# MLP up-projection of an fp32 two-layer trunk: seven half-size products in place of eight, with other SBUF slots and a shorter weight look-ahead

## Chip, cores and metric

One core of one Trainium2 chip runs the whole program in one launch. The metric is the device time of one execution in microseconds (us), the median over runs. Engines are named as in the profile: PE is TensorE's matmul, PEld its weight load, DVE is VectorE, ACT is ScalarE, POOL is GpSimd, SP issues DMAs.

## The reference

512 tokens of width 1024 go through two residual layers: sparse attention with an MLP, then forgetting attention on a shared K/V with an MLP. Everything is float32. The part that matters here is the MLP, which runs once in each layer:

```
D_MODEL = 1024
SEQ = 512
D_FF = 4 * D_MODEL
...
def sq_relu_mlp(xn, w_up, w_down):
    return jnp.square(jax.nn.relu(xn @ w_up)) @ w_down
...
        h = h + sq_relu_mlp(rms_norm(h, g_mlp[layer]), w_up[layer], w_down[layer])
```

## The kernel before, in words

**Arithmetic.** An fp32 operand is split into a high part (rounded to the PE's fp32r format by an ACT copy) and a low part (the rest). A product of two operands is three matmuls, high by high, high by low and low by high (`mm3`, line 521). A weight tile is 1024 words on each of 128 partitions: SP loads it (`raw`), ACT makes `whi` or `dhi`. The low part comes from DVE (raw minus high), or, for the stages listed in `dl`, from ACT (minus the high part) and a DMA from POOL that adds `raw` onto it (`wlo`, lines 507 to 510). The up-projection is in `dl`, the down-projection isn't.

**The MLP** (`mlp`, line 899) goes over four chunks of 1024 hidden features. In a chunk the up-projection makes eight blocks of 128 features by 512 tokens, each in one PSUM bank called `up`: 8 pieces of the width 1024, 3 matmuls each, 24 matmuls with 512 moving columns (`featprod`, line 552). The first four blocks of the first chunk do the same in two halves of 256 tokens, so that they can start before the last tokens are normed. `relu_done` (line 953) makes relu and square on ACT, into four quadrants `X` (256 tokens by 512 features). The down-projection of the chunk multiplies these quadrants by quadrants of `w_down` already with seven products in place of eight (Strassen's scheme in Winograd's form): sums and differences of quadrants on DVE, `dhi`/`dlo` and `xhi`/`xlo` as operands, banks called `tp`, results added into the residual `h` on DVE.

**The order of the work** is written by a list scheduler when the program is built (`schedule`, line 237): each operation has a due time on PE's clock, a table of costs says how long it takes, and the ready operation with the earliest due time goes next on its engine. On the chip each engine then runs its own list in order, and waits on semaphores. A tile takes a slot of SBUF from an arena by its size (`slots` in `CFG`); a weight tile may take one only so many us ahead of PE's clock (`ahead`: raw 40, high 30, low 30).

Of the kernel before, what the change touches and what calls it, by code (L numbers as in the profile page):

```python
# [85 lines left out]
class VTile:  # L86
    _ids = {}

    def __init__(self, pool, shape, dt, name, quota=None):
        n = int(np.prod(shape[1:]))  # L90
        self.words = max(64, 1 << (n - 1).bit_length())

        self.store = pool.arena[self.words] if pool.arena else pool
        self.res = [(p, 1) for p in (self.store, quota) if p is not None]
        self.first = self.end = None
        self.pool, self.shape, self.dt, self.name = pool, tuple(shape), dt, name
        self.real, self.last, self.reads, self.left, self.held, self.by = None, {}, {}, 0, False, {}
# [28 lines left out]
class Recorder:  # L126
# [22 lines left out]
    def add(self, eng, fn, a, k):  # L149
# [21 lines left out]
        if fn == "matmul" and k.get("start"):  # L171
            for p in set(outs[0].t.last.values()):
                op.preds[p] = 1
        for v in outs:
# [62 lines left out]
    def schedule(self):  # L237
# [13 lines left out]
        for o in reversed(ops):  # L251
            for s in o.succ:
                c = (2.0 if o.eng != "POOL" else 5.0) + o.cost if o.fn == "dma_start" else o.cost + self.LAT.get((o.eng, s.eng), 0.1)
                o.prio = min(o.prio, s.prio - c)
# [26 lines left out]
        while done < len(ops):  # L281
# [4 lines left out]
            for e in names:  # L286
# [70 lines left out]
                if o.fn == "dma_start":  # L357
# [3 lines left out]
                    o.end = dma[0] + (1.0 if e != "POOL" else 2.5)  # L361
# [68 lines left out]
def body(ctx, tc, a, out):  # L430
# [14 lines left out]
    def apool(name):  # L445
# [3 lines left out]
        apool(n) for n in ("x8", "h", "wr", "wh", "wl", "s2", "bt", "s4", "ws"))  # L449
    p_ps = pool("ps", 8, bass.MemoryType.PSUM, reach=CFG["ps"])  # L450
    p_dr = {n: pool(n, 1, bass.MemoryType.DRAM) for n in ("hd", "cd")}
# [30 lines left out]
    cosT = const([128, NT, 64], "cosT")  # L482
    sinT = const([128, NT, 64], "sinT")
# [16 lines left out]
    def wunit(src, shape):  # L500
        n = int(np.prod(shape[1:]))
# [90 lines left out]
    def norm_T(src, r, g, xT, t):  # L592
        for i in range(2):
# [6 lines left out]
            c = slice(128 * t, 128 * t + 128)  # L600
            for k in range(2):
                split(xT[0][2 * i + k][:, :, c], xT[1][2 * i + k][:, :, c], b[:, 2 * k:2 * k + 2, :])
# [76 lines left out]
    def unpair(dst, b, scale):  # L679

        up, dn = slice(0, 64), slice(64, 128)
        S.activation(dst[up, 0], b[up], AF.Copy, scale=scale)
# [42 lines left out]
    masks = [scr([128, 128 * (t + 1)], "mask") for t in range(NT)]  # L725
# [85 lines left out]
    oT = new_xT("oT")  # L811
    topk(1)
    qprod(1, 0)
    for t in range(NT):
# [3 lines left out]
        for kv in range(4):  # L818
# [38 lines left out]
            else:  # L857

                pv, u, o = bank([128, 4, 128], "pv"), scr([64, 4, 128], "u"), scr([128, 2, 128], "o")
# [6 lines left out]
            split(oT[0][kv][:, :, c], oT[1][kv][:, :, c], o)  # L866
# [16 lines left out]
    mT = None  # L883

    def proj_o(oT, w, g, first):
        tokprod(xl(oT), w, 0, 8, 0, 512, addto(0), order=first)
        xT = new_xT()

        def last(t, b):
            addto(512)(t, b)  # L890
            norm_T(h[t], rstd(h[t]), g, xT, t)
        tokprod(xl(oT), w, 0, 8, 512, 512, last, order="t")
        return xT

    lows("oa")
    xT = proj_o(oT, a["w_o_a"][0], g, "t")


    def mlp(xT, wu, wd, after, last=False):
        lows("up1" if last else "up0")  # L900
        H = T // 2
        tl = [slice(0, H), slice(H, T)]

        share = [htile([128, 512], "share") for _ in range(2)]

        def add(o, b, x):
            V.tensor_tensor(o, b, x, op=OP.add)

        def xop(src):
            out = []  # L910
            for k in range(0, 4, 2):
                hl = tuple(rec.tile(p_x8, [128, 2, H], F32R, n) for n in ("xhi", "xlo"))
                split(hl[0], hl[1], src[:, k:k + 2, :])
                out.append(hl)
            return out

        def wop(src):
            out = []
            for y in src:
                hl = rec.tile(p_wh, [128, 2, 512], F32R, "dhi"), rec.tile(p_wl, [128, 2, 512], F32R, "dlo")  # L920
                split(hl[0], hl[1], y)
                out.append(hl)
            return out

        def sub(o, p, q):
            for x, y, z in zip(o, p, q):
                V.tensor_tensor(x, y, z, op=OP.subtract)

        def part(b, x, w, start, i, c=slice(0, 512), js=range(2)):

            for j in js:
                for k in (2 * j, 2 * j + 1):
                    mm3(b[:, c], tuple(u[:, k % 2, 128 * i:128 * i + 128] for u in x[j]),
                        tuple(u[:, k % 2, c] for u in w[j]), start and k == 0, k == 3, skip_group_check=True)

        def prod(bs, x, w, start, whole=False):
            if whole:
                for i in range(2):
                    part(bs[i], x, w, start, i)
            else:  # L940
                for j in range(2):
                    for i in range(2):
                        part(bs[i], x, w, start, i, js=(j,))

        def banks():
            return [bank([128, 512], "tp") for _ in range(2)]

        for ci in range(4):
# [11 lines left out]
            if ci == 0:  # L960
                us = [wS(wu, 128 * i) for i in range(4)]
                bs = [bank([128, T], "up") for _ in range(4)]
                for half in range(2):
                    for i in range(4):
                        featprod(xT, us[i], bs[i], tl[half])
# [3 lines left out]
            for f in range(f, 8):  # L969
                b = bank([128, T], "up")  # L970
                featprod(xT, wS(wu, f0 + 128 * f), b)
                relu_done(f, b)


            def raw(j, n):
                ys = []
                for k in range(f0 + 512 * j, f0 + 512 * j + 512, 256):
                    ys.append(rec.tile(p_wr, [128, 2, 512], F32, "raw"))
                    SP.dma_start(ys[-1], wd[k:k + 256, 512 * n:512 * n + 512].rearrange("(k p) c -> p k c", p=128))
                return ys  # L980
# [10 lines left out]
            prod(a, xop(X[0, 0]), w11, True)  # L991
# [5 lines left out]
            prod(a, xop(X[0, 1]), wop(raw(1, 0)), False)  # L997
# [6 lines left out]
            prod(b, xop(s1), wop(y11), True)  # L1004
# [8 lines left out]
            prod(d, xop(s1), wop(y11), True)  # L1013
# [4 lines left out]
            prod(b, xop(X[0, 1]), wop(y22), False, lastc)  # L1018
# [7 lines left out]
            prod(c, xop(X[1, 0]), wop(y12), True)  # L1026
# [5 lines left out]
            x22 = xop(X[1, 1])  # L1032
# [20 lines left out]
    xq, xk = new_xT(), new_xT()  # L1053

    def afterA(t):
# [6 lines left out]
        if t % 2:  # L1062
            c = slice(128 * t - 128, 128 * t + 128)
            for k in range(0, 8, 2):
# [5 lines left out]
                for x, g in ((xq, gq), (xk, gkv)):  # L1070
                    for i in range(2):
                        split(x[0][k // 2][:, i, c], x[1][k // 2][:, i, c], b[:, i, :], scale=g[:, k + i:k + i + 1])

    ys = {}
    mlp(xT, a["w_up"][0], a["w_down"][0], afterA)
# [32 lines left out]
    lows("v")  # L1108

    vb = [[big([128, 8, 2, 64], "vb") for _ in range(2)] for _ in range(NT)]  # L1110
    vbf = {(t, p): htile([128, 128], "vbf") for t in range(NT) for p in CFG["pvb"]}
    for n in range(2):
        def vdone(t, b, n=n):
            for p in CFG["pvb"]:
                if p // 4 == n:
                    S.copy(vbf[t, p], b[:, 128 * (p % 4):128 * (p % 4) + 128])
            split(vb[t][n][:, :, 0, :], vb[t][n][:, :, 1, :], b.heads(64))
        tokprod(xl(xk), wkv, 0, 8, D + 512 * n, 512, vdone)
# [34 lines left out]
    def kproj(p):  # L1153
# [3 lines left out]
        ks = [htile([128, 2, T], "kdup", F32R) for _ in range(2)]  # L1157
        for e in range(2):
# [7 lines left out]
    def bias(hd_):  # L1166
        ck = scr([128, T], "ck")
        SP.dma_start(ck, cd.row(hd_))
        bt = [rec.tile(p_bt, [128, 128 * (t + 1)], F32, "bt") for t in range(NT)]
        for t in range(NT):  # L1170
            n = 128 * (t + 1)
            G.tensor_scalar(bt[t], ck[:, :n], -1.0, cq[:, t, hd_:hd_ + 1], op0=OP.mult, op1=OP.add)
            dg = bt[t][:, n - 128:n]
            G.affine_select(dg, dg, pattern=[[-1, 128]], compare_op=OP.is_ge, fill=NEG, base=0, channel_multiplier=1)
        return bt

    def attn(p, ks, bts):
        pts = {}
        for e in range(2):
# [4 lines left out]
            ls = {}  # L1184
            for t in CFG["bord"]:
# [4 lines left out]
                l, mn = scr([128, n], "l"), small(1, "mn")  # L1190
# [43 lines left out]
        else:  # L1234
            o = scr([128, T], "o")
# [9 lines left out]
        split(qo[p][:, 0, :], qo[p][:, 1, :], o)  # L1245

    kss = {0: kproj(0)}
    bts = {hh: bias(hh) for hh in range(2)}
    for p in range(8):
        if p < 7:  # L1250
            kss[p + 1] = kproj(p + 1)
        attn(p, kss[p], [bts[2 * p], bts[2 * p + 1]])
        if p < 7:
            for hh in (2 * p + 2, 2 * p + 3):
                bts[hh] = bias(hh)
# [8 lines left out]
    def ol(k, t):  # L1264
        return tuple(qo[k][:, i, 128 * t:128 * t + 128] for i in range(2))

    lows("ob")
    tokprod(ol, a["w_o_b"][0], 0, 8, 0, 512, addto(0), order="k")
    xT = new_xT()

    def lastB(t, b):
        addto(512)(t, b)
        norm_T(h[t], rstd(h[t]), g, xT, t)
    tokprod(ol, a["w_o_b"][0], 0, 8, 512, 512, lastB, order="t")
# [21 lines left out]
    mlp(xT, a["w_up"][1], a["w_down"][1], afterB, last=True)  # L1296
# [35 lines left out]
```

## Time and profile before

| | before |
|---|---|
| time, 3 runs | 1168.31 us median (1167.87 to 1169.01) |
| profiled execution | 1168.06 us, of which the span of its instructions 1166.2 us |
| PE busy | 1141.8 us, 98% of the span |
| DVE busy | 771.8 us, 66% |
| ACT busy | 741.6 us, 64% |
| POOL busy | 236.5 us, 20% |
| DMA | 187.86 MB in all, mean 161 GB/s |

A matmul's end is modelled in the profile and successive matmuls overlap, so the price of one in a stream is read from the distance of two starts, and the same holds for DVE and ACT instructions that follow each other at once. All instructions go through one helper, so they stand under one line (L416) and are told apart by tile names, out<-in.

### The profile page before, as it was taken

What the parts mean: (1) busy time and instruction counts of PE and PEld (TensorE: products, weight loads), DVE (VectorE), ACT (ScalarE), POOL (GpSimd) and SP (SyncE); (2) the same over time, 40 slices, a digit from 0 to 9 for tenths busy, and PEclk for the clock granted to TensorE, in tenths of its full rate; (3) what the DMA queues carried; (4) which work ended last, traced back from release to release, by engine and by line L of the source; (5) the groups of instructions that cost most, each with busy time, mean ns of one, the idle gap of its engine ahead of it and who ended that gap; (6) DMA issues with size and microseconds to landing.
All of it is one profiled execution on the core that took longest, in us unless ns stands there. A gap on an engine that the chain in (4) does not pass through costs nothing. (4 is left out here: it accounts for less than half of the span.)

```text
span 1166.2 us, 16382 instructions
## 1 busy us (share of the span) xinstructions
PE 1141.8 (98%) x5687; PEld 948.6 (81%) x5687; DVE 771.8 (66%) x1489; ACT 741.6 (64%) x1396; POOL 236.5 (20%) x391
## 2 busy tenths in 40 slices
PE   8999999999999999999999999999999999999997
PEld 7777787898888888888887878788988888888885
DVE  7899998455736656468656359773568357465596
ACT  8852899665745556559573259996568356465562
POOL 0311454110200200201010068961101002002001
PEclk9999999999999999999999999999999999999999
DMA  9841363782982964957875313768719819739501
GB/s 341 184 91 55 110 181 70 148 235 59 241 242 64 256 186 123 269 150 176 234 173 124 110 37 115 207 169 179 204 68 240 248 56 248 219 88 255 198 19 73
DMA packets 145315, 187.86 MB, mean 161 GB/s; under 512 B 8104, under 2 KB 92096, under 8 KB 145232
## 3 DMA queue, kind: packets, MB, share of 16 engines
q1 hardware_dynamic: 129680, 130.18, 35.5%
q0 software_dynamic: 15552, 56.63, 25.2%
q8 instruction: 45, 0.74, 0.3%
q14 instruction: 38, 0.31, 0.1%
HBM read 125.94 MB, written 4.23 MB: 112 GB/s over the span
## 5 line engine op out<-in xcount | busy, mean ns | idle before, releaser
L416 PE MATMUL up<-xT,whi 128*128 128x512 f32 (+1 forms) x1152 | 323.7, 366 | 0.0
L416 PEld LDWEIGHTS up<-xT,whi 128*128 128x128 f32 x1152 | 207.9, 189 | 34.9
L416 POOL DMA_DIRECT2D wlo<-raw x108 | 95.1, 881 | 692.6 <-ACT wlo L416 339.2
L416 DVE TENSOR_TENSOR dlo<-raw,dhi 128x1024 fp32r<-128x1024 f32 x112 | 136.5, 1227 | 144.5 <-ACT dhi L416 90.3
L416 PE MATMUL up<-xT,wlo 128*128 128x512 f32 (+1 forms) x576 | 210.0, 366 | 0.0
L416 PE MATMUL tp<-dhi,xhi 128*128 128x512 f32 (+1 forms) x452 | 171.9, 390 | 1.2 <-DVE h L416 0.8
L416 PE MATMUL tp<-dlo,xhi 128*128 128x512 f32 (+1 forms) x452 | 171.4, 387 | 0.0
L416 PE MATMUL tp<-dhi,xlo 128*128 128x512 f32 (+1 forms) x452 | 170.8, 388 | 0.0
L416 ACT CAST whi<-raw 128x1024 fp32r<-128x1024 f32 (+2 forms) x124 | 123.9, 1026 | 72.9 <-DMA raw<-in_w_up_dram 63.1
L416 ACT CAST dhi<-raw 128x1024 fp32r<-128x1024 f32 x112 | 116.4, 1047 | 67.1 <-PE up L416 64.1
L416 PE MATMUL tp<-whi,xT 128*128 128x512 f32 (+2 forms) x432 | 125.2, 371 | 2.7 <-DVE r L416 1.6
L416 ACT ACTIVATE wlo<-whi 128x1024 fp32r<-128x1024 f32 x108 | 112.4, 1059 | 20.8 <-DMA wlo<-raw 10.3
L416 PEld LDWEIGHTS up<-xT,wlo 128*128 128x128 f32 x576 | 108.3, 189 | 17.5
L416 DVE TENSOR_TENSOR h<-tp,h 128x512 f32<-128x512 f32 (+1 forms) x97 | 64.7, 680 | 79.0 <-PE tp L416 78.9
L416 PEld LDWEIGHTS tp<-dhi,xhi 128*128 128x128 f32 x452 | 84.8, 188 | 21.7 <-DVE h L416 1.4
L416 PEld LDWEIGHTS tp<-dhi,xlo 128*128 128x128 f32 x452 | 84.7, 188 | 17.3
L416 PEld LDWEIGHTS tp<-dlo,xhi 128*128 128x128 f32 x452 | 84.9, 188 | 16.8
L416 PEld LDWEIGHTS tp<-whi,xT 128*128 128x128 f32 x432 | 77.0, 188 | 14.7 <-ACT whi L416 3.4
L416 DVE TENSOR_TENSOR raw<-raw 128x1024 f32<-128x1024 f32 x64 | 76.6, 1220 | 18.3 <-DMA raw<-in_w_down_dram 17.6
L416 ACT ACTIVATE r<-up 128x512 f32<-128x512 f32 x64 | 37.9, 592 | 79.6 <-PE up L416 79.6
L416 POOL TENSOR_SCALAR l<-l,rc 128x128 f32<-128x128 f32 (+3 forms) x128 | 69.9, 574 | 52.7 <-DVE rc L416 38.3
L416 PE MATMUL tp<-wlo,xT 128*128 128x512 f32 (+2 forms) x216 | 78.4, 372 | 0.5 <-DVE ra L416 0.5
(191 smaller groups left out, 1928.7 us busy)
## 6 DMA issues: line engine op xcount, KB each, us to landing
wlo<-raw POOLq DMA_DIRECT2D x108, 512.0 KB, 8.8
raw<-in_w_down_dram SPq DMA_DIRECT2D x96, 512.0 KB, 10.9
raw<-in_w_up_dram SPq DMA_DIRECT2D x64, 512.0 KB, 7.1
raw<-in_w_kv_b_dram SPq DMA_DIRECT2D x16, 512.0 KB, 6.8
raw<-in_w_in_a_dram SPq DMA_DIRECT2D x12, 512.0 KB, 8.6
raw<-in_w_o_a_dram SPq DMA_DIRECT2D x8, 512.0 KB, 4.4
raw<-in_w_q_b_dram SPq DMA_DIRECT2D x8, 512.0 KB, 7.6
ck<-cd SPq DMA_DIRECT2D x16, 256.0 KB, 3.7
```

Source lines behind the costliest of these rows:

```text
L416: getattr(self.engs[o.eng], o.fn)(*a, **k)
```

## The change

Per MLP, the 28 blocks of the up-projection behind the first four are made four at a time (`quad7`): 512 features by 512 tokens is cut in 2 by 2 by 2, with 256 features, 256 tokens and half of the width 1024, and seven products of that size are made in place of eight. A product is 2 feature blocks, 4 pieces of the width and 3 matmuls, 24 matmuls with 256 moving columns, into one bank. The weights' side needs four sums per quad on DVE (128 x 1024 each) and high and low parts of seven operands in place of four tiles (low parts of three by POOL's DMA, of four by DVE). The tokens' side needs four differences and their high and low parts once per MLP (`tsums`); for these `norm_T` also writes an fp32 copy `xf` of the normed tokens. Results are combined by five DVE additions of 128 x 512 and one ACT copy per quad; the copy after product 1 and the additions after products 6, 5 and 7 read a bank into which the next product then goes on adding.

The SBUF arena has two slot sizes, 44 of 1024 words and 20 of 512, in place of five sizes; small tiles now take a 512 slot, and some are packed together (masks, `l`, the bias tiles of two heads, cos and sin). The MLP's weight tiles may be taken 22 us (raw) and 13 us (high, low) ahead in place of 40 and 30. The scheduler's table lands a DMA 4 us (SP) or 3.5 us (POOL) after its transfer, in place of 1 and 2.5. The new functions `proj7`, `proj_o` and the options `swap` and `dup` are not reached: `p7` is empty and the other two are off.

```
-        self.words = max(64, 1 << (n - 1).bit_length())
+        self.words = 512 if n <= 512 else 1024
...
-    "ahead": {"wr": 40, "wh": 30, "wl": 30},
-    "slots": {1024: 41, 512: 18, 256: 7, 128: 8, 64: 1}, "sizes": (8, 8, 8, 8), "sq": 'S', "x8": 400, "h": 200, "wr": 1500,
+    "land": 4.0, "pw": 700, "p7": (), "swap": False, "dup": False, "ufar": ("1", "2", "4"),
+    "far": ("v3", "v7", "v4"),
+    "mahead": {"wr": 22, "wh": 13, "wl": 13}, "ahead": {"wr": 40, "wh": 30, "wl": 30},
+    "slots": {1024: 44, 512: 20}, "sizes": (8, 8, 8, 8), "sq": 'S', "x8": 400, "h": 200, "wr": 1500,
...
+            split(xT[i, t // 2][0][:, :, c], xT[i, t // 2][1][:, :, c], b)
+            S.copy(xf[i, t // 2][:, :, c], b)
...
+        def tsums():
+            tokside("1", xf[0, 0], xf[0, 1], xf[0, 0])
+            tokside("3", xf[0, 1], xf[1, 1], xf[0, 1])
+            tokside("2", xf[1, 1], xf[1, 1], xf[0, 0])
+            tokside("4", xf[1, 0], xf[1, 0], xf[1, 1])
...
+            def mul(b, w, x, start):
+                for m in range(2):
+                    for k in range(4):
+                        mm3(b[:, H * m:H * m + H], tuple(u[:, k, 128 * m:128 * m + 128] for u in w),
+                            (x(k, 0), x(k, 1)), start and m + k == 0, k == 3, skip_group_check=True)
...
+            mul(b, op(a11, "1"), xd(0, 0), True)
+            m1 = scr([128, T], "r")
+            S.copy(m1, b)
+            a12 = raw(0, 1)
+            mul(b, op(a12, "2"), xd(1, 0), False)
+            done(0, 0, b)
+            s1 = rec.tile(p_mr, [128, 4, 256], F32, "s1")
+            V.tensor_tensor(s1, a21, a22, op=OP.add)
+            V.tensor_tensor(a21, a11, a21, op=OP.subtract)
+            V.tensor_tensor(a11, s1, a11, op=OP.subtract)
+            e = new()
+            mul(e, op(a11, "6"), xs("2"), True)
+            p21 = sumt(e, m1)
+            mul(e, op(s1, "5"), xs("1"), False)
+            p22 = sumt(e, m1)
+            V.tensor_tensor(a12, a12, a11, op=OP.subtract)
+            mul(e, op(a12, "3"), xd(1, 1), False)
+            V.tensor_tensor(m1, e, m1, op=OP.add)
+            done(0, 1, m1)
+            b = new()
+            mul(b, op(a21, "7"), xs("3"), True)
+            V.tensor_tensor(p22, b, p22, op=OP.add)
+            done(1, 1, p22)
+            mul(b, op(a22, "4"), xs("4"), False)
+            V.tensor_tensor(p21, b, p21, op=OP.add)
+            done(1, 0, p21)
...
-            for f in range(f, 8):
-                b = bank([128, T], "up")
-                featprod(xT, wS(wu, f0 + 128 * f), b)
-                relu_done(f, b)
...
+                quad7(f0 + 128 * f, qdone)
```

What this does to the engines' lists shows at three places. The first is PE's list in the up-projection of the first MLP; `up_` with a number is a PSUM bank, `whi`/`uhi` a high part and `wlo`/`ulo` a low part of weights, `xT` and `t` the tokens' side. Before, one block follows the other:

```order
L416 MATMUL up_4076<-xT_2931,wlo_3802 128x512
L416 MATMUL up_4117<-xT_2908,whi_3825 128x512
L416 MATMUL up_4117<-xT_2914,whi_3825 128x512
L416 MATMUL up_4117<-xT_2908,wlo_3835 128x512
L416 MATMUL up_4117<-xT_2908,whi_3825 128x512
```

Now the end of product 6 (bank up_3964) is followed by a piece of product 7 (bank up_4026), and then by the start of product 5, again in bank up_3964:

```order
L423 MATMUL up_3964<-t_3211,uhi_3909 128x256
L423 MATMUL up_3964<-t_3251,uhi_3909 128x256
L423 MATMUL up_3964<-t_3211,ulo_3921 128x256
L423 MATMUL up_4026<-t_3185,uhi_3933 128x256 x2
L423 MATMUL up_4026<-t_3238,uhi_3933 128x256 x2
L423 MATMUL up_4026<-t_3185,ulo_3959 128x256 x2
L423 MATMUL up_4026<-t_3185,uhi_3933 128x256 x2
L423 MATMUL up_4026<-t_3238,uhi_3933 128x256
L423 MATMUL up_3964<-t_3172,uhi_3876 128x256
L423 MATMUL up_3964<-t_3206,uhi_3876 128x256
```

So each matmul is half as wide, and nine matmuls of another product stand between two products that share a bank.

The second place is DVE's list in the same chunk. Before, there is only work of the down-projection:

```order
L416 TENSOR_TENSOR dlo_3515<-raw_3253,dhi_3486 128x1024
L416 TENSOR_TENSOR s1_3541<-sq_3274,sq_3423 128x1024
L416 TENSOR_TENSOR xlo_3552<-sq_3420,xhi_3537 128x512
L416 TENSOR_TENSOR sq_3274<-sq_3267,sq_3274 128x1024
L416 TENSOR_TENSOR xlo_3571<-s1_3541,xhi_3555 128x512
```

Now, for the quad whose banks are shown above, it makes weight sums (`s1`, `raw`), low parts (`ulo`) and the additions out of the banks (`r<-up`):

```order
L423 TENSOR_TENSOR ulo_3959<-raw_3659,uhi_3933 128x1024
L423 TENSOR_TENSOR s1_3974<-raw_3861,raw_3863 128x1024
L423 TENSOR_TENSOR raw_3861<-raw_3784,raw_3861 128x1024
L423 TENSOR_TENSOR raw_3784<-s1_3974,raw_3784 128x1024
L423 TENSOR_TENSOR r_4037<-up_3964,r_3968 128x512
L423 TENSOR_TENSOR xlo_4044<-sq_4013,xhi_4021 128x512
L423 TENSOR_TENSOR ulo_4053<-s1_3974,uhi_4032 128x1024
L423 TENSOR_TENSOR ulo_4067<-raw_3784,uhi_4048 128x1024
L423 TENSOR_TENSOR raw_3806<-raw_3806,raw_3784 128x1024
L423 TENSOR_TENSOR r_4094<-up_3964,r_3968 128x512
```

The addition `r_4037<-up_3964` is what product 5 waits for, and it stands in line behind three sums of 1024 words.

The third place is DVE's list at the end of the program, where `v`, `r` and `hg` are the final norm of two finished token blocks. Before:

```order
L416 TENSOR_TENSOR h<-tp,h 128x512 x2
L416 TENSOR_TENSOR hg<-h,g 128x512
L416 TENSOR_TENSOR v<-ss 128x1
L416 TENSOR_TENSOR hg<-h,g 128x512
L416 TENSOR_TENSOR v<-ss 128x1
L416 TENSOR_SCALAR v<-v 128x1 x2
L416 SCALAR_TENSOR_TENSOR v<-v 128x1 x2
L416 TENSOR_SCALAR v<-v 128x1 x2
L416 TENSOR_TENSOR r<-v 128x1 x2
L416 TENSOR_SCALAR hg<-hg,r 128x512 x2
L416 TENSOR_TENSOR h<-tp,h 128x512
```

Now the last product's low parts stand behind that norm:

```order
L423 SCALAR_TENSOR_TENSOR v<-v 128x1 x2
L423 TENSOR_SCALAR v<-v 128x1 x2
L423 TENSOR_TENSOR r<-v 128x1 x2
L423 TENSOR_SCALAR hg<-hg,r 128x512 x2
L423 TENSOR_TENSOR dlo<-raw,dhi 128x1024
L423 TENSOR_TENSOR xlo<-sq,xhi 128x512
L423 TENSOR_TENSOR dlo<-raw,dhi 128x1024
L423 TENSOR_TENSOR xlo<-sq,xhi 128x512
L423 TENSOR_TENSOR h<-tp,h 128x512
```

Two `dlo` and two `xlo` moved from ahead of the norm to behind it.

## Rows read from the trace of the kernel before

**Rows 1.** The page: span, and busy time, share and instructions of each engine.

```profile
span 1166.2 us, 16382 instructions
...
PE 1141.8 (98%) x5687; PEld 948.6 (81%) x5687; DVE 771.8 (66%) x1489; ACT 741.6 (64%) x1396; POOL 236.5 (20%) x391
```

**Rows 2.** Chain that ended last, second MLP: start us, us, what.

```profile
872.95 37.73 PE tp L416 x166
...
911.59 43.07 PE up L416 x190
```

**Rows 3.** PE's up-projection by shape: count, busy us, mean ns, idle before.

```profile
L416 PE MATMUL up<-xT,whi 128*128 128x512 f32 x896 | 276.9, 389 | 0.0
L416 PE MATMUL up<-xT,wlo 128*128 128x512 f32 x448 | 174.3, 389 | 0.0
L416 PE MATMUL up<-xT,whi 128*128 128x256 f32 x256 | 46.8, 284 | 0.0
```

**Rows 4.** Timeline of PE, first four blocks of the second MLP.

```profile
834.80 0.40 PE L416 MATMUL up<-xT,whi 128*128 128x256 f32 x2
...
845.24 0.40 PE L416 MATMUL up<-xT,whi 128*128 128x256 f32 x2
```

**Rows 5.** Weight loads of the up-projection, all shapes of matmul together.

```profile
L416 PEld LDWEIGHTS up<-xT,whi 128*128 128x128 f32 x1152 | 207.9, 189 | 34.9
```

**Rows 6.** Engines in three chunks of the second MLP (first, third, last and end).

```profile
832.00:911.00 79.00, 79.00 (x426) 68.50 (x425) 48.35 (x57) 47.36 (x72) 6.12 (x7) 1.00 0.70 183
993.00:1075.00 82.00, 82.00 (x363) 67.65 (x362) 47.83 (x54) 46.87 (x68) 7.00 (x8) 1.00 0.69 184
1075.00:1166.00 91.00, 82.21 (x371) 67.60 (x369) 60.55 (x92) 42.45 (x84) 6.75 (x5) 0.98 0.32 103
```

**Rows 7.** Timeline of DVE, instructions of one kind that follow each other.

```profile
394.95 1.28 DVE L416 TENSOR_TENSOR h<-tp,h 128x512 f32<-128x512 f32 x2
...
433.57 3.49 DVE L416 TENSOR_TENSOR raw<-raw 128x1024 f32<-128x1024 f32 x3
```

**Rows 8.** DVE and ACT groups by shape: busy us, mean ns, idle before.

```profile
L416 DVE TENSOR_TENSOR raw<-raw 128x1024 f32<-128x1024 f32 x64 | 76.6, 1220 | 18.3 <-DMA raw<-in_w_down_dram 17.6
L416 DVE TENSOR_TENSOR h<-tp,h 128x512 f32<-128x512 f32 x95 | 63.8, 686 | 79.0 <-PE tp L416 78.9
...
L416 ACT CAST whi<-raw 128x1024 fp32r<-128x1024 f32 x116 | 118.8, 1046 | 72.9 <-DMA raw<-in_w_up_dram 63.1 <-DVE h L416 4.9 <-DMA wlo<-raw 2.1
```

**Rows 9.** Timeline: a bank read by DVE, and PE going on in it.

```profile
1145.40 0.61 PE L416 MATMUL tp<-dhi,xlo 128*128 128x512 f32 x2
...
1145.83 1.29 DVE L416 TENSOR_TENSOR h<-tp,h 128x512 f32<-128x512 f32 x2 [2.07 <-PE tp L416]
...
1156.24 0.41 DVE L416 TENSOR_TENSOR h<-tp,h 128x256 f32<-128x256 f32 x1
...
1156.71 0.39 PE L416 MATMUL tp<-dhi,xhi 128*128 128x256 f32 x1 [0.83 <-DVE h L416]
```

**Rows 10.** DMA issues: count, KB each, median us from issue to landing.

```profile
wlo<-raw POOLq DMA_DIRECT2D x108, 512.0 KB, 8.8
raw<-in_w_down_dram SPq DMA_DIRECT2D x96, 512.0 KB, 10.9
raw<-in_w_up_dram SPq DMA_DIRECT2D x64, 512.0 KB, 7.1
```

**Rows 11.** Engines in two stretches outside the MLPs (first attention, second attention).

```profile
100.00:200.00 100.00, 99.08 (x542) 78.16 (x542) 93.80 (x288) 81.08 (x208) 44.11 (x74) 1.00 0.40 109
...
700.00:790.00 90.00, 87.90 (x503) 72.43 (x502) 75.00 (x202) 87.45 (x211) 72.04 (x154) 1.00 0.58 165
```

**Rows 12.** Timeline of DVE at the end, behind the final norm of two token blocks.

```profile
1150.47 0.68 DVE L416 TENSOR_TENSOR h<-tp,h 128x512 f32<-128x512 f32 x1
...
1152.89 0.69 DVE L416 TENSOR_TENSOR h<-tp,h 128x512 f32<-128x512 f32 x1 [1.02 <-PE tp L416]
...
1154.72 0.69 DVE L416 TENSOR_TENSOR h<-tp,h 128x512 f32<-128x512 f32 x1 [0.41 <-PE tp L416]
```

More of the change, by code (lines that the diff above doesn't have):

```diff
@@ L173, in add @@
                 op.preds[p] = 1
+        if fn == "matmul":
+            t = outs[0].t
+            if k.get("start"):
+                t.begun = op
+            elif t.begun is not None:
+                op.preds[t.begun] = 1
         for v in outs:
@@ L882, in body, with add, xop, pieces @@
     g = gain(a["g_mlp"][0])
[L883 to L887, printed above, removed]
+    def add(o, b, x):
+        V.tensor_tensor(o, b, x, op=OP.add)
+    def xop(src):
+        out = []
+        for x in src:
+            hl = tuple(rec.tile(p_x8, [128, 2, H], F32R, n) for n in ("xhi", "xlo"))
+            split(hl[0], hl[1], x)
+            out.append(hl)
+        return out
+    def pieces(x):
+        return [x[:, 0:2, :], x[:, 2:4, :]]
@@ new lines, in wop, with each @@
+    def wop(src, far=False):
+        out = []
+        for y in src:
+            hl = rec.tile(p_mh, [128, 2, 512], F32R, "dhi"), rec.tile(p_ml, [128, 2, 512], F32R, "dlo")
+            if far:
+                S.copy(hl[0], y)
+                S.activation(hl[1], f32(hl[0]), AF.Copy, scale=-1.0)
+                G.dma_start(hl[1], y, accum_op=OP.add)
+            else:
+                split(hl[0], hl[1], y)
+            out.append(hl)
+        return out
+    def each(op, o, p, q):
+        for x, y, z in zip(o, p, q):
+            V.tensor_tensor(x, y, z, op=op)
@@ new lines, in sub, with part, prod @@
+    def sub(o, p, q):
+        each(OP.subtract, o, p, q)
+    def part(b, x, w, start, i, c=slice(0, 512), js=range(2)):
+        for j in js:
+            for k in (2 * j, 2 * j + 1):
+                mm3(b[:, c], tuple(u[:, k % 2, 128 * i:128 * i + 128] for u in x[j]),
+                    tuple(u[:, k % 2, c] for u in w[j]), start and k == 0, k == 3, skip_group_check=True)
+    def prod(bs, x, w, start, whole=False):
+        if whole:
+            for i in range(2):
+                part(bs[i], x, w, start, i)
+        else:
+            for j in range(2):
+                for i in range(2):
+                    part(bs[i], x, w, start, i, js=(j,))
@@ L889, in last, with proj_d @@
+    quad = lambda x: {(i, j): [x[2 * j + k][:, :, tl[i]] for k in range(2)] for i in range(2) for j in range(2)}
+    def proj_d(lhs, w, g, order):
+        tokprod(lhs, w, 0, 8, 0, 512, addto(0), order=order)
+        xT, xf = new_xq()
         def last(t, b):
             addto(512)(t, b)
[L891 to L899, printed above, removed]
-        lows("up1" if last else "up0")
-        H = T // 2
-        tl = [slice(0, H), slice(H, T)]
-        share = [htile([128, 512], "share") for _ in range(2)]
[L906 to L946, printed above, removed]
@@ L1053, in body @@
     xq, xk = new_xT(), new_xT()
+    xv = [big([128, 2, T], "xv", F32) for _ in range(4)] if "v" in CFG["p7"] else None
     def afterA(t):
@@ L1262, in body, with ol @@
     g = gain(a["g_mlp"][1])
[L1264 to L1274, printed above, removed]
+    if oB:
+        xT, xf = proj_o(quad(oB), a["w_o_b"][0], g, "ob")
+    else:
+        def ol(k, t):
+            return tuple(qo[k][:, i, 128 * t:128 * t + 128] for i in range(2))
+        lows("ob")
+        xT, xf = proj_d(ol, a["w_o_b"][0], g, "k")
     gl = {}
```

281 lines of the change are left out of this document (225 added, 56 removed).

## Prediction

> **What bounds the kernel now.** I read the page first: PE is busy for 1141.8 of 1166.2 us, 98%, while DVE stands at 66% and ACT at 64% [rows 1]. A busy PE need not be a full PE, so the second view is the chain that ended last: in the second MLP it is PE alone, 43.07 us of 190 up-projection matmuls and 37.73 us of 166 down-projection matmuls [rows 2]. That is 0.2267 and 0.2273 us per matmul of 512 columns, back to back. The windows agree: PE fills all of a chunk's 82 us, DVE 47.8 and ACT 46.9 of them [rows 6]. So in the MLPs time is the number of matmuls by their distance, and whatever takes matmuls away shortens the chunk, as long as no other engine grows past it.
>
> **What the change removes.** The trace has 896 + 448 = 1344 up-projection matmuls of 512 columns [rows 3]; all of them lie in the blocks that are rewritten, 14 quads of four blocks (14 x 4 x 24 = 1344). At 0.2267 us they take 304.7 us.
>
> **What it adds on PE.** A quad now has 7 products of 24 matmuls of 256 columns, so 14 x 168 = 2352. The price of one is in this trace, because the first four blocks are made in halves of 256 tokens by the same three-matmul helper, with a weight load for each matmul. In the second MLP a run of them shows high, high, low in a steady beat: from the start at 834.80 to that at 845.24 there are 29 such triples, 87 matmuls, in 10.44 us [rows 4], so 0.1200 us each. 2352 x 0.1200 = 282.2 us. The saving is 22.4 us. It is much less than the eighth that the count of multiplications promises (38 us), because half a matmul costs 53% of a whole one. The point from which it saves nothing is 304.7 / 2352 = 0.1296 us, only 8% above the price.
>
> That margin makes the weight load the first thing to doubt. A load is 189 ns long in the rows [rows 5], longer than the 120 ns of a half-size matmul, yet in [rows 4] every matmul has its load and the beat stays at 0.120, so loads are hidden there, and the new products have the same sequence of loads and widths. The Trainium skill, "TensorE: Matmul & The Clock Gate", in Part 3 under "What overlaps and what doesn't", says that a weight load overlaps matmuls in flight only when it goes to other rows of the array, which full 128-row weights never do. By it the loads would lie bare, twice as many of them, and the change would lose; [rows 2, 4] do not agree with it, and the sum goes by the rows.
>
> **What it adds elsewhere.** DVE: per quad four sums and four low parts of 1024 words and five additions of 512. Those that follow each other start (3.49 - 1.22) / 2 = 1.135 and 1.28 - 0.68 = 0.60 us apart [rows 7, 8], so 8 x 1.135 + 5 x 0.60 = 12.1 us a quad, 24.2 us a chunk. By the whole duration of a row (1.220 and 0.686, [rows 8]) it would be 26.4 us; that is the upper bound, and the lower value is the one that a busy line pays. A middle chunk becomes 82 - 2 x 1.6 = 78.8 us long, with 47.8 + 24.2 = 72.0 us of DVE (91%; 94% by the upper bound). The first chunk, with one quad and the tokens' four differences and low parts (8 x 1.135 = 9.1 us), comes to 48.4 + 12.1 + 9.1 = 69.6 of 77.4 us [rows 6]. ACT: per quad three more casts (1.05 us, [rows 8]), one negation less and a bank copy of about 0.6, so at most 7.5 us a chunk, 54.4 of 78.8. POOL has one DMA less per quad. None of them passes PE, so I book them at nothing, with PE as their cover; DVE's cover is thin, and it is the first rival below.
>
> Turnarounds: four times a quad a bank is read between two products that add into it. From [rows 9], the read starts 0.43 us after the start of the bank's last matmul (the first of the two at 1145.40, to 1145.83), takes about 0.69 [rows 8], and PE starts 0.06 after its end (1156.65 to 1156.71): the price is 0.95 us behind the 0.23 of the matmul itself. PE's list has at least nine half-size matmuls of another product in that place, 1.08 us, so 0.13 us is left where DVE is free at once. I take 1 us in all for those of the 56 turnarounds where it isn't (lower bound nothing; upper bound in the rivals).
>
> Look-ahead: a raw weight lands 7.1 or 10.9 us after its issue, POOL's addition 8.8 [rows 10]. 22 and 13 us ahead still cover one landing each; the DMA traffic doesn't grow. I book nothing.
>
> The end: two `dlo` and two `xlo` now stand behind the final norm of two token blocks, 2 x 1.135 + 2 x 0.60 = 3.5 us more between the first addition at 1145.83 and the last product's additions. DVE idles there for 1.02 + 0.41 = 1.43 us [rows 12], so PE gets its last operands about 2.0 us later, and at the end nothing hides that: 2.0 us lost. Bounds: 0 if PE's other work reaches that far, 3.5 if the idle time isn't usable.
>
> Outside the MLPs the matmuls stay the same; slots and due times shift the order. PE lacks 0.9 of 100 us in the first attention and 2.1 of 90 in the second [rows 11], so there is little to win; a loss of the same size, twice over, is my bound: -3 to +5, taken as 0.
>
> **The sum**, against the profiled execution's own 1168.06 us (span 1166.2 and 1.9 around it): -22.4 + 1.0 + 2.0 = -19.4, so 1148.7. The median of the runs lies 0.25 above that execution, so I forecast 1149 us.
>
> **The rivals.**
> - *DVE becomes the bound.* At 91 to 94% it has 4.6 to 6.8 us a chunk to spare, and it runs its list in order: an addition out of a bank that comes ready while a 1024-word sum runs waits up to 1.14 us for it, and PE then waits as well. There are 3 x 14 = 42 turnarounds through DVE; if each is late by that, 48 us go and the time is about 1197. It decides from 19.4 / 42 = 0.46 us on average. For it: the list shows `r<-up` right behind three such sums. Against it: 9% is idle, and PE's list has matmuls of another product in every turnaround.
> - *Weights come late.* If the shorter look-ahead lets a ninth of a landing of 8.8 us show in each quad, 1 us, 14 us go: about 1163. For it: raw weights now go through a DVE sum before their casts. Against: in the trace PE has no wait for weights in the MLP, and 22 us is twice the longest landing.
> - *The loads show.* If a half-size matmul can't go below its load's 189 ns [rows 5], 2352 x 0.189 = 444.5 us, 140 more than before: 1308. That is also what the Trainium skill's rule would come to, in kind. Against: the beat of [rows 4].
> - *The saving doesn't arrive in full, by many small waits,* half of it lost: about 1158.
> - *The other stages gain*, by 3 us or more, from DMAs issued earlier and more large slots: below 1143.
>
> **How the numbers follow.** The sum, with its bounds (0 to 3.5 at the end, 0 to 3 at the turnarounds, -3 to +5 elsewhere), holds 1143 to 1155: chance 0.68. Half or more of the saving lost to late DVE or late weights, 1155 to 1166: 0.17; nearly all of it, within 0.2% (2.3 us, about what a measurement of this kernel can tell from no change): 0.03. Slower: 0.07, of which DVE as the bound 0.05, the loads 0.01 and weights 0.01. Below 1143: 0.05. So faster 0.90, the same 0.03, slower 0.07. The range takes the likeliest case and the near part of the second: 1142 to 1160.
>
> **What would show it.** Right: an `up` group of 2352 matmuls of 256 columns whose starts are 0.120 us apart, PE without idle time in the middle chunks, a chunk of about 79 us, DVE about 72 us busy in it, and PE waiting for DVE once near the end by about 2 us. Wrong: PE idle in the MLP with `r<-up` or `ulo` on DVE as its releaser (the first rival), or with `raw` or `ulo` landings (the second), or a beat above 0.130 (the third).

## The result, and the profile after

The changed kernel takes 1158.77 us (median of 4 runs, 1157.49 to 1160.14) beside 1168.55 for the kernel before in the same session: a ratio of 0.9916, 95% interval 0.9904 to 0.9928. That is 9.8 us faster, half of the 19.4 that the prediction's sum gave, and inside its range. The profiled execution is the slowest of the four, 1160.14 us.

The page of the kernel after, beside [rows 1]:

```profile
span 1158.3 us, 18559 instructions
...
PE 1126.7 (97%) x6695; PEld 981.4 (85%) x6695; DVE 958.7 (83%) x1671; ACT 788.3 (68%) x1390; POOL 225.2 (19%) x377
```

DVE has 187 us more to do, PE 15 us less. The up-projection by shape, beside [rows 3] (count, shortest, median and longest ns, first and last start), and two starts from PE's timeline:

```profile
L423 PE MATMUL up<-t,uhi x896: 277/283/387, 269.0 to 1104.5; 128*128 128x256 f32 x180
L423 PE MATMUL up<-xT,uhi x672: 277/283/387, 266.1 to 1099.8; 128*128 128x256 f32 x168
L423 PE MATMUL up<-t,ulo x448: 278/283/283, 269.2 to 1104.8; 128*128 128x256 f32 x150
L423 PE MATMUL up<-xT,ulo x336: 274/283/283, 266.4 to 1100.1; 128*128 128x256 f32 x168
```

```profile
1097.30 0.64 PE L423 MATMUL up<-xT,uhi 128*128 128x256 f32 x4
...
1100.17 0.40 PE L423 MATMUL up<-t,ulo 128*128 128x256 f32 x2
```

The four counts add up to 2352. Between the two starts lie 24 matmuls in 2.87 us, 0.1196 each: the forecast price. The second MLP in four windows, each from the first `up` of a chunk to that of the next, the last to the end of the program, and then three windows of 4 us near the end (columns as in [rows 6]):

```profile
821.08:898.17 77.09, 77.09 (x514) 71.09 (x512) 71.47 (x83) 55.18 (x81) 4.36 (x5) 1.00 0.60 167
898.17:977.34 79.17, 79.00 (x506) 71.90 (x505) 70.82 (x80) 51.50 (x67) 5.25 (x6) 1.00 0.64 173
977.34:1056.60 79.26, 79.13 (x505) 71.92 (x504) 71.61 (x81) 51.40 (x67) 5.22 (x6) 1.00 0.65 173
1056.60:1158.30 101.70, 87.26 (x541) 78.10 (x539) 87.30 (x120) 54.86 (x91) 10.21 (x8) 0.95 0.37 109
...
1132.00:1136.00 4.00, 3.01 (x14) 2.16 (x12) 3.55 (x7) 2.70 (x6) 0.00 (x0) 1.00 0.00 0
1136.00:1140.00 4.00, 2.09 (x7) 1.24 (x7) 4.00 (x15) 1.87 (x6) 0.00 (x0) 1.00 0.30 112
1140.00:1144.00 4.00, 3.89 (x12) 3.06 (x12) 3.60 (x6) 0.00 (x0) 0.00 (x0) 0.57 0.43 155
```

The two middle chunks take 79.2 us, where the same starts were 81.76 us apart before, and DVE is busy for 70.8 and 71.6 of them. In the window to the end PE stands still for 14 us, and the granted clock is 0.95. PE's waits (us in all, times, longest), of which all but the second belong to the MLPs:

```profile
PE up L423 <- DVE r L423: 2.7, 5, 1.1
PE tp L423 <- DVE r L423: 1.8, 1, 1.8
...
PE tp L423 <- DVE dlo L423: 1.6, 1, 1.6
...
PE tp L423 <- DVE v L423: 1.3, 1, 1.3
...
PE tp L423 <- DVE h L423: 0.5, 1, 0.5
```

The second was there before as well, with 1.6 us. PE waits for DVE twice near the end (`v`, `dlo`), and right behind that it runs 4 us at a granted clock of 0.57, near the lower of its two levels (1.2 of 2.4 GHz): 12 matmuls there instead of 18 (4 / 0.227).

Where the two executions differ, by the starts of the first and last matmuls of a stage:

| stretch | before, us | after, us | difference | forecast |
|---|---|---|---|---|
| start to the first `up` | 240.32 | 242.12 | +1.8 | 0 |
| from there to the first `up` of the second MLP | 585.56 | 578.96 | -6.6 | -10.7 |
| from there to the last matmul | 332.24 | 326.56 | -5.7 | -8.7 |
| last matmul to the last instruction | 8.01 | 10.62 | +2.6 | 0 |

The forecast column shares the 22.4 and the 1.0 us of the sum evenly and puts the 2.0 us of the end in the third row. The +1.8 in the first row differs from execution to execution: a kernel below (end_order) whose lists are the same up to the first MLP reached it at 240.26. The work isn't shared out quite as before either: behind the program's last `up` 149 matmuls of 512 columns start where 156 did, so 1.6 us of the end's work (7 x 0.227) now lie further ahead.

### The profile page after: what moved, and what is told of

Read it like the earlier page. It is cut to its first block, busy times and chain, and to the rows that moved or that the text cites. A ratio compares the mean times of both kernels' runs of the same rounds, so it can differ in the third digit from the quotient of the medians.

```text
span 1158.3 us, 18559 instructions
## 1 busy us (share of the span) xinstructions
PE 1126.7 (97%) x6695; PEld 981.4 (85%) x6695; DVE 958.7 (83%) x1671; ACT 788.3 (68%) x1390; POOL 225.2 (19%) x377
## 5 line engine op out<-in xcount | busy, mean ns | idle before, releaser
L423 PE MATMUL up<-t,uhi 128*128 128x256 f32 x896 | 146.4, 283 | 0.1
L423 POOL DMA_DIRECT2D ulo<-raw x42 | 36.7, 873 | 526.1 <-ACT ulo L423 336.5
L423 PEld LDWEIGHTS up<-t,uhi 128*128 128x128 f32 x896 | 126.1, 192 | 0.9 <-DVE r L423 0.3
L423 PE MATMUL up<-xT,uhi 128*128 128x256 f32 x672 | 117.7, 284 | 2.7 <-DVE r L423 2.7
L423 DVE TENSOR_TENSOR raw<-raw 128x1024 f32<-128x1024 f32 x92 | 110.6, 1218 | 4.0 <-DMA ulo<-raw 3.3
L423 PEld LDWEIGHTS up<-xT,uhi 128*128 128x128 f32 x672 | 99.8, 191 | 4.9 <-DVE r L423 3.9
L423 PE MATMUL up<-t,ulo 128*128 128x256 f32 x448 | 95.2, 283 | 0.0
L423 ACT CAST uhi<-raw 128x1024 fp32r<-128x1024 f32 x84 | 85.1, 1047 | 13.4 <-DVE raw L423 8.1
L423 PE MATMUL up<-xT,ulo 128*128 128x256 f32 x336 | 80.7, 283 | 0.0
L423 POOL DMA_DIRECT2D wlo<-raw x52 | 45.8, 917 | 170.8 <-ACT wlo L423 105.6
```

The costliest lines, as they stand in the source:

```text
L423: getattr(self.engs[o.eng], o.fn)(*a, **k)
```

## The experiments

All times are medians; ratios are to the kernel before in the same session, with 95% intervals.

| run | what it is | us | ratio |
|---|---|---|---|
| slots_only | whole blocks; new slots, table and look-ahead | 1178.38 | 1.0088 [1.0073, 1.0103] |
| slots_long | the same, look-ahead 40/30/30 | 1168.84 | 1.0003 [0.9994, 1.0011] |
| slots_land | as slots_only, old table of landings | 1179.58 | 1.0096 [1.0082, 1.0110] |
| half_blocks | eight blocks in halves, nothing else | 1192.69 | 1.0207 [1.0190, 1.0224] |
| no_turn | products, each in its own bank | 1155.47 | 0.9890 [0.9875, 0.9905] |
| land_old | products, old table | 1160.46 | 0.9932 [0.9918, 0.9945] |
| ahead16 | products, 22/16/16 | 1154.71 | 0.9883 [0.9870, 0.9897] |
| ahead_long | products, 40/30/30 | 1230.53 | 1.0530 [1.0515, 1.0546] |
| dve_all16 | ahead16, all low parts on DVE | 1153.97 | 0.9870 [0.9854, 0.9885] |
| end_order | products, final norm behind the last operands | 1158.89 | 0.9915 [0.9900, 0.9929] |
| end_far16 | ahead16, four low parts off DVE at the end of both MLPs | 1154.35 | 0.9880 [0.9864, 0.9897] |
| last_far16 | the same in the second MLP only | 1149.95 | 0.9847 [0.9833, 0.9860] |

**Whole blocks: what slots, table and look-ahead cost without the products.** The kernel after with the old loop in place of `quad7`, on `norm_T` and `featprod` as before:

```
-                quad7(f0 + 128 * f, qdone)
+                for i in range(f, f + 4):
+                    b = bank([128, T], "up")
+                    featprod(xT, wS(wu, f0 + 128 * i, pools=(p_mr, p_mh, p_ml)), b)
+                    relu_done(i, b)
```

> The changed kernel with the up-projection as eight whole blocks per chunk of 512 columns, as before, but with the new slots, table of landings and 22/13/13 us look-ahead. Prediction's step (slots, table and look-ahead cost nothing): 1168.5 us, within 1.5. Theory (the new order costs about 3 us outside the MLPs): 1170.5 to 1173 us, with PE's waits in the two attentions as in the changed kernel and none in the MLPs. Rival (the short look-ahead itself makes weights late): above 1174 us with PE waits for whi or wlo in the MLPs.

It took 1178.38 us, 10 more than before, and neither the zero nor the 3 us was right. The rival has the time (above 1174) but not the sign: in the MLPs PE has no wait for `whi` or `wlo`, only one for a `dlo` at the end:

```profile
PE tp L423 <- DVE dlo L423: 2.7, 1, 2.7
```

Its trace shows the loss at the two entries into an MLP (2.6 us each against slots_long below; the first isn't clear of the 1.9 us by which executions of one order differ there, 242.12 and 240.26 above) and at the end (7.0). Two more kernels take the three settings apart:

```
-    "mahead": {"wr": 22, "wh": 13, "wl": 13}
+    "mahead": {"wr": 40, "wh": 30, "wl": 30}
```

> The kernel with whole blocks, new slots and new table (the run of 1178.4 us, 10 above before), with the MLP's weight look-ahead set back to 40, 30 and 30 us. Theory L (the short look-ahead leaves DVE no lead, so that it is late at the end of the last chunk): the end gets back its 6 us, 1171 to 1174 us. Theory T (the table of landings, by the order it gives) and theory S (the slots): no change, 1177 to 1180 us.

```
-    "land": 4.0            (and 6.0, 3.5 for POOL)
+    "land": 1.0            (and 5.0, 2.5 for POOL)
```

> The same kernel with whole blocks and new slots at 22, 13 and 13 us, but with the table of landings set back to 1 us for SP and 2.5 us for POOL. Theory T: most of the 10 us comes back, 1169 to 1172 us, most of it in the second attention and at the end. Theories L and S: 1177 to 1180 us.

slots_long is at 1168.84, the time of before; slots_land stays at 1179.58. So with whole blocks and the long look-ahead slots and table cost nothing, and the short look-ahead costs 9.5 us in these slots. (These runs change the lead of `raw` and that of the high and low parts together.) How, the windows of the last chunk show, slots_only first (DVE is the third of the busy times):

```profile
1090.00:1100.00 10.00, 10.00 (x46) 8.29 (x45) 0.69 (x1) 5.16 (x9) 1.75 (x2) 1.00 1.06 308
1100.00:1110.00 10.00, 10.00 (x46) 8.29 (x45) 0.69 (x1) 3.75 (x8) 0.00 (x0) 1.00 0.46 134
...
1130.00:1140.00 10.00, 10.00 (x46) 8.26 (x45) 10.00 (x13) 6.26 (x12) 1.89 (x1) 1.00 0.00 0
1140.00:1150.00 10.00, 10.00 (x46) 8.28 (x45) 10.00 (x11) 2.11 (x2) 2.41 (x2) 1.00 0.00 0
1150.00:1160.00 10.00, 7.78 (x32) 5.49 (x31) 9.80 (x24) 4.08 (x11) 0.00 (x0) 1.00 0.01 2
```

and slots_long, whose chunk starts 4 us earlier:

```profile
1086.00:1096.00 10.00, 10.00 (x46) 8.29 (x45) 6.46 (x6) 6.62 (x11) 0.00 (x0) 1.00 0.79 271
1096.00:1106.00 10.00, 10.00 (x46) 8.29 (x45) 7.23 (x7) 5.84 (x11) 0.00 (x0) 1.00 0.30 103
...
1136.00:1146.00 10.00, 10.00 (x46) 8.29 (x45) 4.70 (x8) 0.00 (x0) 2.54 (x2) 1.00 0.00 0
1146.00:1156.00 10.00, 10.00 (x46) 7.97 (x45) 7.02 (x20) 3.24 (x10) 1.40 (x2) 1.00 0.28 104
```

With 13 us DVE is nearly idle (0.69 of 10 us) in the first part of the chunk's up-projection, since the scheduler may not place the down-projection's low parts yet; then it is full for 30 us, and PE waits 2.7 us for a `dlo`. Of the program's last 14 `dlo` eight start behind the last `up`, in slots_long two. The work is the same; it is only too late.

**The price of a half-size matmul.**

```
-                quad7(f0 + 128 * f, qdone)
+                for i in range(f, f + 4):
+                    u, b = wS(wu, f0 + 128 * i, pools=(p_mr, p_mh, p_ml)), bank([128, T], "up")
+                    for half in range(2):
+                        for k in range(8):
+                            mm3(b[:, tl[half]], (u[0][:, k, :], u[1][:, k, :]),
+                                tuple(x[:, k % 4, :] for x in xT[k // 4, half]), k == 0, k == 7)
+                    relu_done(i, b)
```

> The changed kernel with eight blocks per chunk made in two halves of 256 tokens each: 2688 half-size matmuls, no sums, no combination. Price 0.120 us each: 322.6 us where before took 304.7, so 17.9 us above before, 1186 us, if nothing else costs anything, and 1189 us with the 3 us of the other stages. Rival (weight loads hold a half-size matmul back when they come in a long run): 0.189 us each, over 1350 us.

1192.69 us: 14.3 above slots_only, which has the same settings, where 17.9 were forecast for 2688 half-size in place of 1344 whole matmuls. From the first to the last `up` of the second MLP it takes 299.84 us where slots_only took 290.77, 9.1 more with 9.0 forecast; the first MLP gives 9.1 as well. The stretches ahead of the two MLPs' first `up` are 3.7 us shorter than in slots_only, which is why the whole shows less. Half-size matmuls that follow each other start 0.120 us apart in its trace (median over its 3072), so the price is right and a long run of loads doesn't hold it back:

```profile
L423 PEld LDWEIGHTS up<-xT,whi 128*128 128x128 f32 x2048 | 317.5, 189 | 0.6
```

The load is still 189 ns in the row. The rule of the Trainium skill, "TensorE: Matmul & The Clock Gate", Part 3, "What overlaps and what doesn't", by which such loads would lie bare, isn't borne out by this trace. From here to the changed kernel the eighth product's 336 matmuls go, 40.3 us; measured are 33.9, and 38.0 to ahead16 below, which has a longer look-ahead than this one.

**Turnarounds, table and look-ahead with the products.** In no_turn four products start in a bank of their own:

```
-            mul(e, op(s1, "5"), xs("1"), False)
+            e = new()
+            mul(e, op(s1, "5"), xs("1"), True)
...                        (the same for products 2, 3 and 4)
```

> The changed kernel with products 2, 5, 3 and 4 of a quad each started in a bank of its own instead of going on in the bank of the product before; the same matmuls, additions, copies and transfers, but no product waits until DVE or ACT has read a bank. The sums lack the terms of the earlier product, so part of the up-projection's result is left out. Theory 1 (PE's 7 us of waits for DVE r in the MLPs are the bank turnarounds): they vanish, 1152 to 1155 us. Theory 2 (they show a DVE that is late because it itself waits for the transfer that makes a low part, and PE would wait for the next operand in their place): PE waits for ulo or raw instead, 1157 to 1160 us.

1155.47 us, 3.3 less. PE's waits for `r` in the MLPs are gone, and no wait for operands stands in their place; at the end PE waits 4.2 us for `h`. Theory 1 holds for the place, but its size wasn't 7 us: the rows of PE's waits give 2.7, and by the starts of the new products' matmuls, where each that comes later than 0.15 us behind the one before is counted with what it is above 0.12, it is 5.1 us in the changed kernel and nothing here. That DVE is late because it waits for a transfer, the first half of Theory 2, is also so, as the next run but one shows.

> The changed kernel, products and all, with only the table of landings set back to 1 and 2.5 us. Theory T: 3 to 6 us come back in the stages outside the MLPs and at the end, 1152 to 1156 us. Theory L: no change there, 1157 to 1160 us. Rival (the table's later landings are what gives the products' operands their lead): PE waits in the MLPs grow, above 1161 us.

land_old (the table's edit above, on the changed kernel) took 1160.46: nothing came back, and nothing in the MLPs got worse. Theory T is out in both kernels.

```
-    "mahead": {"wr": 22, "wh": 13, "wl": 13}
+    "mahead": {"wr": 22, "wh": 16, "wl": 16}
```

> The changed kernel with the high and low parts of the MLP's weights 16 us ahead instead of 13. Theory L: some of PE's waits for DVE in the MLPs and at the end go, 1153 to 1156 us. Theories T and S: 1157 to 1160 us.

1154.71 us: three microseconds more lead give 4.1 us back, and the rows of waits for `r` are gone with every turnaround in its place; by the starts, 1.3 of the 5.1 us are left. So a turnaround by itself costs little: DVE came late to it. Why, the trace of the changed kernel shows, here at the longest of the waits, with its page's row for such sums first:

```profile
L423 DVE TENSOR_TENSOR raw<-raw 128x1024 f32<-128x1024 f32 x92 | 110.6, 1218 | 4.0 <-DMA ulo<-raw 3.3
...
328.10 0.88 POOL L423 DMA_DIRECT2D ulo<-raw  x1 [3.21 <-ACT ulo L423]
...
338.35 1.23 DVE L423 TENSOR_TENSOR raw<-raw 128x1024 f32<-128x1024 f32 x1 [1.21 <-DMA ulo<-raw]
339.49 0.68 DVE L423 TENSOR_TENSOR r<-up,r 128x512 f32<-128x512 f32 x1
340.23 0.74 PE L423 MATMUL up<-xT,uhi 128*128 128x256 f32 x4 [1.09 <-DVE r L423]
```

A sum that overwrites a `raw` tile has to wait until POOL's transfer has read that tile for a low part; the transfer was issued 10.2 us before. The addition `r` stands behind the sum in DVE's list, and PE waits for it. All five waits for `r` have this chain, with DVE idle for the transfer 1.21, 0.34, 0.80, 0.28 and 0.65 us (the 3.3 us of the page's row). With three microseconds more lead two sums in the first quads still wait for a transfer, 0.8 us in all, and no wait of PE stands behind them. No run at 13 us makes these low parts without transfers, which would test the chain alone; order and times in the trace, and ahead16, are what shows it. DVE's load isn't what makes it late: at most other turnarounds of the changed kernel it is early, and in the second MLP it stands idle ahead of an `r`, until PE is done with the bank, 11 times for 17.1 us in all (4 times for 3.8 in ahead16). The chunks of ahead16, in the same windows as above, and two of 4 us near its end:

```profile
819.92:896.78 76.86, 76.86 (x513) 70.99 (x512) 70.71 (x82) 54.68 (x81) 4.37 (x5) 1.00 0.60 173
896.78:975.78 79.00, 79.00 (x505) 71.81 (x504) 70.30 (x80) 51.37 (x67) 5.19 (x6) 1.00 0.62 172
975.78:1054.62 78.84, 78.84 (x505) 71.76 (x504) 71.50 (x82) 52.12 (x67) 5.30 (x7) 1.00 0.63 174
1054.62:1152.20 97.58, 85.33 (x541) 76.80 (x539) 87.97 (x121) 53.88 (x89) 9.73 (x7) 0.97 0.39 114
...
1132.00:1136.00 4.00, 2.18 (x10) 1.39 (x9) 3.87 (x15) 2.00 (x8) 0.00 (x0) 1.00 0.25 94
1136.00:1140.00 4.00, 3.94 (x22) 3.06 (x21) 4.00 (x7) 0.11 (x1) 0.00 (x0) 1.00 0.46 173
```

A middle chunk is now PE alone, 78.8 to 79.0 us, where 78.8 were forecast. At the end PE still waits for DVE `h`, 1.8 and 0.7 us, and DVE is full there.

> The changed kernel with the MLP's weights 40, 30 and 30 us ahead as before. Theory L alone (more lead is better): 1150 to 1155 us. Theory with slots (a quad holds four raw tiles and up to seven pairs of operands, more than four whole blocks did, so that a long lead takes the slots that others wait for): long waits of PE for weights, above 1170 us.

The other direction (40, 30, 30) took 1230.53 us. The middle chunks of the second MLP are 114.7 and 93.7 us long; in the first of them PE is busy for 102.9 and DVE for 92.7 us, and over the program PE waits most for operands:

```profile
PE tp L423 <- DVE dlo L423: 24.1, 32, 1.5
PE up L423 <- DMA ulo<-raw: 6.0, 4, 2.0
PE up L423 <- DVE r L423: 5.8, 6, 1.5
```

The same 40, 30, 30 cost nothing with whole blocks. That up-projection operands hold the slots that the down-projection's `dlo` needs fits both, but no row shows a slot; it is argued, not shown.

**Is DVE the bound?** In ahead16, `"ufar": ()` in place of `("1", "2", "4")`:

> The changed kernel at 16 us with all seven low parts of a quad on DVE instead of four: 3 x 1.135 = 3.4 us more per quad, 6.8 per chunk, which brings DVE from about 73 to 79.8 us in a chunk of 78.8. First rival of the prediction (DVE becomes the bound when its slack is gone): chunks of about 80 us and PE waiting for DVE, 1160 to 1175 us. Against it (the transfer that a low part takes is what was late, and DVE at its limit still keeps PE fed): within 2 us of 1154.7 us.

1153.97 us, the same time. From the first to the last `up` of the second MLP:

```profile
817.46:1098.21 280.75, 280.62 (x1884) 259.81 (x1882) 274.30 (x305) 173.21 (x233) 0.00 (x0) 1.00 0.41 136
```

DVE is busy for 274.3 of 280.75 us, 98%, and PE misses 0.13 us. With lead enough, a DVE that is nearly full costs PE nothing. (The run also takes POOL's transfers for `ulo` away, so DVE has nothing to wait for there.)

**The end.** end_order writes the norm of the first two token blocks behind the last product's operands:

```
             for i in range(2):
                 addh(i, 1, b[i])
-                if lastc:
-                    after(i)
...
             w4 = wop(y21)
+            for i in range(2 if lastc else 0):
+                after(i)
```

> The changed kernel with one edit: the final norm of the first two token blocks is written behind the operands of the last product, so that DVE makes its two dlo and two xlo ahead of the norm. Theory (the changed kernel loses about 7 us at its end because PE waits 1.31 and 1.59 us for DVE there and then runs a stretch at a granted clock of 0.57): both waits and the low clock vanish, 1152 to 1155 us. Rival (the norm only moves to the tail, or the clock falls for another reason): the tail grows by what PE saves, 1157 to 1160 us.

1158.89 us, no change. The waits for `v` and `dlo` are gone, but one for DVE `h` stands in their place:

```profile
PE tp L423 <- DVE h L423: 3.8, 1, 3.8
```

The profiled execution is the fastest of its four, 1155.78 us, with an end 3.0 us shorter than the changed kernel's (50.6 us from the last `up` to the last instruction, beside 53.5); the other three took 1158.57 to 1159.72, so that "no change" rests on the times and not on this trace. This other order doesn't help: DVE has too much left to do. So end_far16 takes work away, on top of ahead16:

```
-            prod(c, xop(pieces(X[1, 0])), wop(y12), True)
+            prod(c, xop(pieces(X[1, 0])), wop(y12, far=lastc), True)
...
-            w4 = wop(y21)
+            w4 = wop(y21, far=lastc)
```

> The changed kernel with high and low parts 16 us ahead, and in the last chunk of each MLP the low parts of the down-projection's last two operands come from ACT and a POOL transfer instead of DVE, 4 x 1.135 = 4.5 us less for DVE at the end. Theory (DVE, full from 1120 to 1142 us in the run at 16 us, is what PE waits for there, 1.8 and 0.7 us, and what delays the last additions by 2 us): 1150 to 1153 us. Rival (the transfers land too late, or the tail is set by the norm's own chain): 1154 to 1157 us.

1154.35 us, no change in all, but from two parts that cancel. From the last `up` to the last instruction it takes 47.0 us, where ahead16 takes 51.0: the forecast 4 us. Between the MLPs (start of the last chunk of the first to the first `up` of the second) it takes 347.9, where ahead16 takes 343.7. There PE waits 2.3 us for DVE `h` and the granted clock falls:

```profile
560.00:570.00 10.00, 7.73 (x37) 6.47 (x36) 4.05 (x8) 5.45 (x8) 0.87 (x1) 0.83 0.91 265
```

The last run keeps the edit for the second MLP alone (`far=lastc and last`):

> The changed kernel at 16 us, with the last two down-projection operands' low parts by ACT and POOL in the last chunk of the second MLP only (the run before did it in both MLPs, gained 4.0 us at the program's end and lost 4.0 between the MLPs, where PE waited 2.3 us for DVE h and the granted clock was 0.83 in the 10 us around). If the two places are independent: 1154.7 less 4.0, 1150 to 1152 us. Rival (the gain at the end needs the other order): 1153 to 1156 us.

1149.95 us, the fastest of all, 18 us below before. Its last window, from the start of the last chunk, beside 97.58 in ahead16 and 101.70 in the changed kernel:

```profile
1053.17:1146.70 93.53, 84.97 (x541) 76.90 (x539) 80.52 (x117) 57.20 (x93) 17.11 (x11) 0.97 0.52 141
```

## Why the prediction was right, and where it was off

- **The saving on PE, 22.4 us: right.** 2352 matmuls at 0.1196 us, PE alone in a chunk as soon as operands come in time (78.8 to 79.0 us at 16 us). The row of the first blocks was the right place to read the price.
- **DVE's load, 72.0 us of a chunk booked at nothing: right.** 70.8 and 71.6 measured, and dve_all16 shows that even 98% costs nothing. The first rival falls as a bound. Its sign did show, PE idle with `r<-up` on DVE as its releaser, but for 2.7 us in all where it priced 48, and each time DVE was late because of a transfer.
- **Turnarounds, 1.0 us: mis-sized, 2.7 us** of PE waits for `r`, 5.1 by the starts of matmuls. The cause isn't the bank alone but DVE's late arrival at it, since in ahead16 the same turnarounds cost 1.3 us by the starts, near the forecast.
- **Look-ahead, "I book nothing": the step that failed.** The prediction compared 22 and 13 us with one landing of a DMA and looked for PE's own waits, which is the wrong measure. In the changed kernel no engine waited for a landing of `raw`; but within the 13 us a cast, a negation and POOL's transfer have to be done before a sum in DVE's list may overwrite the tile, and where the transfer took 10.2 us the additions behind that sum came late. With whole blocks, which have no such sums, the look-ahead works in another way: it also says how early ACT and DVE may make operands, and DVE's idle time in a chunk's first half can't be used if it is short. It costs 9.5 us with whole blocks, and 4.1 us with products from 16 to 13 us. So the rival of late weights had the right edit and, with products, half of the mechanism: a landing does show, though through DVE's list and with less than its 14 us.
- **The end, 2.0 us: mis-sized.** From the last `up` to the last instruction before took 48.35 us and the changed kernel 53.5, 5.1 more, with seven matmuls fewer to do. At 16 us it is 2.7 more (three matmuls fewer), near the forecast; the other 2.5 went with the longer look-ahead, about 1.7 of them being the low clock of this one execution (last section). The prediction counted DVE's four moved operands and found PE's waits for them (1.3 and 1.6 us), but neither the granted clock behind these waits nor the 2.6 us that DVE's late additions add to the tail after the last matmul.
- **Other stages, 0: right within what one execution tells.** slots_long, with new slots and table and the old look-ahead, has the time of before.

In all, 1158.8 lies 9.8 us above the point, at the time of the fourth rival (half of the saving lost). Small waits at the turnarounds, which that rival had, are a part of it, the end is another: 4.1 us come back with the look-ahead (ahead16) and 4.8 with less DVE work at the end (last_far16). With both the kernel is at 1149.95. That this is the forecast's 1149 is luck: the last edit makes the end 1.4 us shorter than before's, so it gives more than the change had lost there, and the kernel before wasn't run with it. The span of its profiled execution is 19.5 us shorter than before: 9.2 and 10.7 in the two up-projection stretches (first to last `up` of an MLP), 1.4 behind the second and 0.2 ahead of the first, less 2.0 us lost between the MLPs. What costs these 2.0 us stays open; slots_long, with whole blocks, loses 2.1 there in its one profiled execution, so that it need not be the products.

## What to carry to other kernels

A limit on how early a buffer may be taken is a limit on every engine that fills it, not on the DMA alone: look whether the filling engine stands idle in the stretch before and is full in the stretch behind. In a list that runs in order, an instruction that waits for a transfer holds up all that stands behind it: look what waits behind a tile that is overwritten. An engine at 98% needn't cost anything if its work may be done early, and one at 83% costs several microseconds if it may not. At the end of this program taking work off the full engine helped, and reordering it only moved the wait.

## What was not expected of the hardware

The granted clock fell to 0.57 for the 4 us behind two idle times of PE of 1.3 and 1.6 us in the changed kernel. Two starts from its timeline, five matmuls of 512 columns apart:

```profile
1141.22 0.63 PE L423 MATMUL tp<-dhi,xlo 128*128 128x512 f32 x1
...
1143.36 0.63 PE L423 MATMUL tp<-dlo,xhi 128*128 128x512 f32 x1
```

That is 0.43 us each in place of 0.227. In ahead16 two waits of 1.8 and 0.7 us at the same place left the clock at 1.00 (its last two rows above). land_old has nearly the same two waits as the changed kernel, and its clock stayed at 1.00 as well:

```profile
PE tp L423 <- DVE dlo L423: 1.6, 1, 1.6
PE tp L423 <- DVE v L423: 1.5, 1, 1.5
...
1140.00:1144.00 4.00, 2.25 (x9) 1.29 (x8) 4.00 (x7) 0.93 (x2) 0.00 (x0) 1.00 0.70 262
1144.00:1148.00 4.00, 3.30 (x22) 2.91 (x23) 4.00 (x7) 1.67 (x6) 0.96 (x1) 1.00 0.02 4
```

So 2.9 us of waits cost 1.7 us more (4 x 0.43) in the one execution, and 3.1 us of them nothing more in the other; from the last `up` to the last instruction land_old takes 51.9 us, 1.6 less than the changed kernel. What tells the two apart, these runs don't show, nor whether the changed kernel's other three executions had the low clock.
